# GpSimd's arithmetic of the first two layers is given to VectorE and ScalarE

## The chip, the cores and the metric

The kernel runs on one core of one Trainium2 chip. The metric is the device time of one execution in microseconds. Three runs of the kernel before took 1056.38, 1057.58 and 1059.24 us; the median is 1057.58 us.

## The reference, cut to what matters

Four layers work one after the other on x of 256 rows and 1024 columns, all in fp32. The first layer holds stick-breaking attention and a grouped state-space mixer (S5), the second a gated linear attention (GLA) in chunks of 64 rows; the third and fourth are hybrid layers with dilated attention and retention, which the change doesn't touch. What matters of the first two:

```
# layer 1: S5, 32 groups of 16 channels, 64 complex states each
lam_bar = exp(lam * dt)
b_bar   = ((lam_bar - 1) / lam)[..., None] * (b_re + i b_im)
bu      = einsum('gnp,blgp->blgn', b_bar, u)
h[t]    = lam_bar * h[t-1] + bu[t]                       # over 256 rows
y       = einsum('gpn,blgn->blgp', c_re, h.real) - einsum(..., c_im, h.imag) + d * u
y       = gelu(y);  y = y * sigmoid(y @ w_glu + b_glu)
x       = x + concat(o_sticks * silu(z_a), y * silu(z_b)) @ w_out
# layer 2: GLA, 4 heads, chunks of 64 rows
g       = cumsum(log_a, over the chunk);  g_last = g[-1]
q_dec, k_inv, k_dec = q * exp(g), k * exp(-g), k * exp(g_last - g)
o       = mask(q_dec k_inv^T) v + q_dec S;   S = exp(g_last) * S + k_dec^T v
```

## The kernel before, in words

**Projections.** Weights come from one array `in_wall_dram` in tiles of 128 by 2048 (1 MB, tile name raw, three buffers), in the order in which they are used. ScalarE copies each to a rounded fp32r tile (whi), VectorE takes the difference to the original (wlo, four pieces of 512 columns), and TensorE multiplies with both parts: `proj_a` sums 512-wide results (pa) from whi, wlo, whi per 128 rows of weights, `proj_b` 512- and 256-wide ones (pb), evacuated by ScalarE and VectorE together (zz, s_room). So every projection needs all three engines, and whi and wlo tiles have three buffers each.

**S5.** The mixer is worked in four pieces of eight groups (`s5_piece`, L1112), four rows to a step, so that a scan of 64 steps does it. First `s5_prep` makes small tables of 32 columns (s_w, s_W, s_L), and per piece angles, their sines and cosines (parts of s_room, the big S5 tile). `s5_tables` (L1080) loads 256 KB of b and c for the piece (s5bc) and makes f0 (s5f), ez and F from W, L and s5bc by `s5_tab`, two products of 256 columns each, and rho for the scan. TensorE transposes ez (s5ep), ScalarE evacuates it (s5E), TensorE makes the input states (s5vp) and a 90 degree turn (s5jp), VectorE rotates, scans (s5B) and rotates back (s5V, s5m), TensorE turns again (s5jp) and gives the outputs (s5yp). Beside it, s5gp, s5f and s5tp make the taps within four rows. The tables have one buffer each, so those of a piece follow the use of the piece before. When all four are done, 32 small DMAs on SyncE's queue gather the result (s_room<-s5Y).

**GLA.** `q_evac` and `k_evac` (L1540 and on) scale q and k by the decays (qd, kc, ki, km) and prepare copies of parts of them for the chunk borders (qi, and parts of kc and km). When all four are ready, TensorE transposes kc (gkt) and goes on with the heads.

**Order.** Fibers yield instructions; `Prog.run` always issues the one with the smallest modelled start plus the fiber's bias, so that the order of every engine is fixed when the program is built. The model's costs are in `Engine.__getattr__` (L295 to L306): a VectorE product of n columns 0.066 + 0.00104 n us, a GpSimd one 0.05 + 0.0021 n us. GpSimd's and VectorE's instructions have no effect on each other in it. On an engine the instructions run in that order, each waiting for its inputs. In the trace every instruction has line L275, so the tiles' names tell what it is.

Of the kernel before, what the change touches and what calls it, by code (L numbers as in the profile page):

```python
# [11 lines left out]
AF = mybir.ActivationFunctionType  # L12
OP = mybir.AluOpType
# [3 lines left out]
P = 128  # L17
T = 256
# [945 lines left out]
def s5_prep(g, ev, S):  # L964

    act, dve, pool, C = g.act, g.dve, g.pool, g.C
    big = ev.tile([P, 20, 32], F32, name="s5_w")
    n = [0]

    def tl():  # L970
        n[0] += 1
        return big[:, n[0] - 1, :]

    def tt(o, a, b, op=OP.mult):
        return dve.tensor_tensor(o, a, b, op=op)

    def ts(o, a, s1, s2, op0, op1=None):
        return dve.tensor_scalar(o, a, s1, s2, op0=op0, **({"op1": op1} if op1 else {}))

    lre, lim = C("lre"), C("lim")  # L980
    dt, a, th = tl(), tl(), tl()
    yield act.activation(dt, C("ldt"), AF.Exp)
    yield tt(a, lre, dt)
    yield tt(th, lim, dt)
    q, p = tl(), tl()
    r, kk = tl(), tl()
    yield from reduce_angle(g, r, th, kk)
    sn, cm1 = tl(), tl()
    f = tl()
    yield ts(f, r, 4.0 / TWO_PI, None, OP.mult)  # L990
    yield ts(kk, f, MAGIC, MAGIC, OP.add, OP.subtract)
    yield tt(f, f, kk, OP.subtract)

    jv = g.K("misc")[:, 0:64]
    flat = lambda t, b: t[:, 8 * b:8 * b + 8, :].rearrange("p a j -> p (a j)")

    def turns():
        for b in range(4):
            gs = slice(8 * b, 8 * b + 8)
            yield pool.tensor_tensor(S.cosj[:, gs, :], f[:, gs].unsqueeze(2).to_broadcast([P, 8, 64]),  # L1000
                                     jv.unsqueeze(1).to_broadcast([P, 8, 64]), op=OP.mult)
        for b in range(4):
            yield ts(flat(S.sinj, b), flat(S.cosj, b), MAGIC, MAGIC, OP.add, OP.subtract)
            yield tt(flat(S.cosj, b), flat(S.cosj, b), flat(S.sinj, b), OP.subtract)
            yield act.activation(flat(S.sinj, b), flat(S.cosj, b), AF.Sin, scale=TWO_PI_BELOW)
            yield act.activation(flat(S.cosj, b), flat(S.cosj, b), AF.Abs)
            yield act.activation(flat(S.cosj, b), flat(S.cosj, b), AF.Sin, scale=-TWO_PI_BELOW, bias=g.halfpi)
            g.flags.add(("turns", b))
        yield from rotary_tables(g)
    yield act.activation(sn, r, AF.Sin)  # L1010
    yield act.activation(cm1, r, AF.Sin, scale=0.5)
    g.spawn(turns(), 0.05)
    yield ts(q, a, -88.0, 1.0 / 256.0, OP.max, OP.mult)
    yield ts(p, q, 1.0 / 6.0, 1.0, OP.mult, OP.add)
    for i in (5, 4, 3, 2):
        yield tt(p, p, q)
        yield ts(p, p, 1.0 / i, 1.0, OP.mult, OP.add)
    yield tt(p, p, q)
    for _ in range(8):
        yield dve.scalar_tensor_tensor(p, p, 2.0, p, op0=OP.add, op1=OP.mult)  # L1020
    em1, ea, cs = p, tl(), tl()
    yield ts(ea, em1, 1.0, None, OP.add)
    yield dve.scalar_tensor_tensor(cm1, cm1, -2.0, cm1, op0=OP.mult, op1=OP.mult)
    yield ts(cs, cm1, 1.0, None, OP.add)
    xr, xi = tl(), tl()
    rho, lr1, den, u, v = S.rho, tl(), tl(), tl(), tl()
    yield tt(xr, em1, cs)
    yield tt(xi, ea, sn)
    yield tt(xr, xr, cm1, OP.add)
    yield tt(lr1, ea, cs)  # L1030
    yield tt(rho, ea, ea)
    yield tt(u, lre, lre)
    yield tt(rho, rho, rho)
    yield tt(v, lim, lim)
    L, Wt = S.L, S.W
    yield dve.tensor_copy(L[:, 0, :, 0], lr1)
    yield dve.tensor_copy(L[:, 1, :, 0], xi)
    yield tt(den, u, v, OP.add)
    yield dve.reciprocal(den, den)
    u2, v2 = tl(), tl()  # L1040
    yield tt(u, xr, lre)
    yield tt(v, xi, lim)
    yield tt(u2, xi, lre)
    yield tt(v2, xr, lim)
    yield tt(u, u, v, OP.add)
    yield tt(u2, u2, v2, OP.subtract)
    yield tt(Wt[:, 0, :, 3], u, den)
    yield tt(Wt[:, 1, :, 3], u2, den)

    def cmul(o, i):  # L1050

        j = i - 1 if o is L else i + 1
        ar, ai = o[:, 0, :, j], o[:, 1, :, j]
        yield tt(u, ar, lr1)
        yield tt(v, ai, xi)
        yield tt(u2, ar, xi)
        yield tt(v2, ai, lr1)
        yield tt(o[:, 0, :, i], u, v, OP.subtract)
        yield tt(o[:, 1, :, i], u2, v2, OP.add)

    for k in (2, 1, 0):
        yield from cmul(Wt, k)

    yield ts(Wt[:, 1], Wt[:, 1], g.sg, None, OP.mult)
    g.flags.add("s5W")
    for k in (1, 2, 3):
        yield from cmul(L, k)
    yield ts(L[:, 0], L[:, 0], g.sg, None, OP.mult)
    g.flags.add("s5L")


def s5_tab(g, bc, m, w, c):

    for a in range(2):
        w4 = w.rearrange("p (q a) t -> p q a t", a=2)[:, :, a, :].unsqueeze(3).to_broadcast([P, 4, 4, 16])
        b4 = bc[:, c, :].rearrange("p (q a c) -> p q a c", q=4, a=2)[:, :, a, :].unsqueeze(2).to_broadcast([P, 4, 4, 16])
        yield g.pool.tensor_tensor(m(a), w4, b4, op=OP.mult)


def s5_tables(g, S):  # L1080

    pool = g.pool
    for b in range(4):
        gs = slice(8 * b, 8 * b + 8)
        bc = yield from g.get("s5bc", [P, 4, P])
        yield g.sp.dma_start(out=bc, in_=g.A["s5bc"][b])
        ez = yield from g.get("s5ez", [P, 512])
        f0 = yield from g.get("s5f0", [P, P])
        yield pool.tensor_scalar(f0, bc[:, 2, :], g.sg, None, op0=OP.mult)
        if "s5W" not in g.flags:  # L1090
            yield g.on("s5W")
        m = yield from g.t2k("s5t")
        half = lambda t: lambda a: t.rearrange("p (q t a c) -> p q t a c", q=4, t=4, a=2)[:, :, :, a, :]
        yield from s5_tab(g, bc, half(ez), S.W[:, 0, gs, :], 0)
        yield from s5_tab(g, bc, half(m), S.W[:, 1, gs, :], 1)
        yield pool.tensor_tensor(ez, ez, m, op=OP.subtract)
        S.ez[b] = (ez, f0)
        rho = yield from g.get("s5rho", [P, 8, 64])
        yield pool.tensor_tensor(rho, S.rho[:, gs].unsqueeze(2).to_broadcast([P, 8, 64]),
                                 g.K("misc")[:, 64:128].unsqueeze(1).to_broadcast([P, 8, 64]), op=OP.mult)  # L1100
        if "s5L" not in g.flags:
            yield g.on("s5L")
        own = lambda t: lambda a: t.rearrange("p (q a t c) -> p q a t c", q=4, t=4, a=2)[:, :, a]
        F = yield from g.get("s5F", [P, 512])
        yield from s5_tab(g, bc, own(F), S.L[:, 0, gs, :], 2)
        yield from s5_tab(g, bc, own(m), S.L[:, 1, gs, :], 3)
        yield pool.tensor_tensor(F, F, m, op=OP.subtract)
        g.put(m, bc)
        S.fr[b] = (F, rho)


def s5_piece(g, S, Y, b):  # L1112

    act, dve, pool, pe = g.act, g.dve, g.pool, g.pe
    U = S.U
    gs = slice(8 * b, 8 * b + 8)
    r3 = lambda t: t.rearrange("p (a j) -> p a j", a=8)
    if b not in S.ez:
        yield lambda: b in S.ez
    ez, f0 = S.ez[b]  # L1120
# [5 lines left out]
    for a in range(2):  # L1126
        yield act.activation(E[:, :, a, :], ep.rearrange("p (q n) -> p q n", q=4), AF.Copy,
                             scale=g.half[:, a:a + 1])
# [43 lines left out]
    F, rho = S.fr[b]  # L1172
    yield dve.tensor_tensor_scan(B, rho.rearrange("p a j -> p (a j)"), B, 0.0, OP.mult, OP.add)
    g.put(rho)
    yield dve.tensor_tensor(r3(V), sb, r3(B), op=OP.mult)
    yield pool.tensor_tensor(r3(m), cb, r3(B), op=OP.mult)
    g.put(B)
    jp = yield from g.ps1("small", "s5jp")
    yield pe.matmul(jp, g.K("jt"), V, start=True, stop=True)
# [293 lines left out]
def odd_layer(g, od):  # L1473
# [73 lines left out]
    def q_evac(j):  # L1547
        def evac(o):
            sl = slice(2 * j, 2 * j + 2)
            if "eg" not in g.flags:  # L1550
                yield g.on("eg")
            yield dve.scalar_tensor_tensor(fl(qd[:, sl]), o, P ** -0.5, fl(eg[:, sl]), op0=OP.mult, op1=OP.mult)
            g.put(o)
            if "ed" not in g.flags:
                yield g.on("ed")
            yield pool.tensor_copy(qi[:, sl, 0:64], qd[:, sl, P:P + 64])
            for i in (2 * j, 2 * j + 1):
                yield pool.tensor_scalar(qi[:, i, 64:128], qd[:, i, P + 64:T], egl[:, 4 * i + 2:4 * i + 3], None, op0=OP.mult)
            ready.add(("q", j))
        return evac  # L1560

    def k_evac(j):
        def evac(o):
# [8 lines left out]
            yield dve.tensor_tensor(km[:, sl, :, 0:64], o4[:, :, :, 0:64], e4[:, sl, :, 0:64], op=OP.mult)  # L1572
            g.put(o)
            for i in (2 * j, 2 * j + 1):
                yield pool.tensor_scalar(kc[:, i, 0:64], kc[:, i, 0:64], egl[:, 4 * i + 1:4 * i + 2], None, op0=OP.mult)
            yield pool.tensor_copy(km[:, sl, :, 64:128], ki.rearrange("p h (a t) -> p h a t", a=2)[:, sl, :, 64:128])
            ready.add(("k", j))
        return evac
    yield from g.proj_a(g.ha, [[("ov", nb, kt) for kt in range(2)] for nb in range(2)],
# [427 lines left out]
```

## Time and profile before

| | |
|---|---|
| runs, us | 1056.38, 1057.58, 1059.24 |
| profiled execution, us | 1061.02 |
| its span, first to last instruction, us | 1059.2 |
| mean granted TensorE clock | 0.988 |
| TensorE matmuls busy, us | 1025.7 (97%), 5507 |
| VectorE busy, us | 823.5 (78%), 1807 |
| ScalarE busy, us | 556.2 (53%), 935 |
| GpSimd busy, us | 69.0 (7%), 79 |

Busy times are unions of an engine's instructions. [...] PE is TensorE, PEld its weight loads, DVE VectorE, ACT ScalarE, POOL GpSimd, SP SyncE, whose q stands for the queue that issues DMAs. An fp32 matmul shows as two. [...] GpSimd is busy only in the first 143 us and for some us around 300.

### The profile page before, as it was taken

Reading aid. Unit: us, or ns where it says so; the run is one execution under the profiler, and the core shown is the slowest. Engines: PE = TensorE matmul, PEld = TensorE weight load, DVE = VectorE, ACT = ScalarE, POOL = GpSimd, SP = SyncE. Lnnn points to the kernel's source line nnn. Section 1 sums busy time; section 2 is a strip of 40 time slices with the busy share of each in tenths; the row PEclk is TensorE's granted clock in tenths of the full one; section 3 lists DMA queues with packets and bytes.
Section 4 is the critical chain, followed back from the end, with each engine's and each line's share of the span. In section 5 each row is a group of like instructions: output and inputs, shape, how many; then the busy total and the mean of one; then the engine's idle time right before and its main releaser. Section 6 shows DMA issues by size and latency. Waiting matters only on the chain.

```text
span 1059.2 us, 14771 instructions
## 1 busy us (share of the span) xinstructions
PE 1025.7 (97%) x5507; PEld 863.3 (81%) x5507; DVE 823.5 (78%) x1807; ACT 556.2 (53%) x935; POOL 69.0 (7%) x79
## 2 busy tenths in 40 slices
PE   9978999999999999999999999999999999999997
PEld 7756777877888778888888888878888888888885
DVE  7997466977789867867599989676676759996775
ACT  7636347755645655445544556555454454455552
POOL 0266410000030000000000000000000000000000
PEclk9998899999999999999999999999999999999999
DMA  8522124454663767564444577545655453454541
GB/s 330 175 93 90 50 88 133 170 183 169 265 247 127 261 251 287 207 243 164 161 153 155 179 259 271 175 150 204 234 189 204 144 187 143 149 182 176 199 179 41
DMA packets 33492, 192.36 MB, mean 182 GB/s; under 512 B 8171, under 2 KB 9195, under 8 KB 11148
## 3 DMA queue, kind: packets, MB, share of 16 engines
q1 hardware_dynamic: 33132, 190.90, 50.1%
q8 instruction: 43, 0.70, 0.3%
q10 hardware_dynamic: 288, 0.52, 0.1%
q14 instruction: 29, 0.24, 0.1%
HBM read 189.31 MB, written 1.05 MB: 180 GB/s over the span
## 4 chain that ended last, share of the span: by engine, by line
PE 77%; DVE 12%; DMA 3%; ACT 2%; issue 2%; POOL 1%; SPq 1%; POOLq 0%; DVEq 0%; ACTq 0%
PE pb L275 46%; PE pa L275 19%; DVE wlo L275 4%; PE as L275 4%; DMA raw<-in_wall_dram 2%; PE ret L275 2%; DVE rs L275 2%; SPq L275 1%; PE sbz L275 1%; PE s5yp L275 1%; ACT whi L275 1%; PE ntp L275 1%; DVE s_w L275 1%; DVE s_room L275 1%; PE gsc L275 0%
## 5 line engine op out<-in xcount | busy, mean ns | idle before, releaser
L275 DVE TENSOR_TENSOR wlo<-raw,whi 128x512 fp32r<-128x512 f32 x604 | 399.2, 697 | 94.4 <-ACT whi L275 94.4
L275 PE MATMUL pb<-H,whi 128*128 128x512 f32 x1344 | 470.0, 400 | 0.0
L275 PE MATMUL pb<-H,wlo 128*128 128x256 f32 x1344 | 353.7, 283 | 0.0
L275 ACT ACTIVATE whi<-raw 128x1024 fp32r<-128x1024 f32 x302 | 304.7, 1052 | 73.8 <-PE pa L275 38.6
L275 PEld LDWEIGHTS pb<-H,whi 128*128 128x128 f32 x1344 | 242.6, 188 | 46.4 <-issue 1.5
L275 PEld LDWEIGHTS pb<-H,wlo 128*128 128x128 f32 x1344 | 253.6, 189 | 15.7 <-issue 0.7
L275 PE MATMUL pa<-whi,H 128*128 128x512 f32 x576 | 184.4, 397 | 2.1 <-DVE H L275 2.1
L275 PEld LDWEIGHTS pa<-whi,H 128*128 128x128 f32 x576 | 108.1, 189 | 26.6 <-DVE H L275 3.5
L275 PE MATMUL pa<-wlo,H 128*128 128x512 f32 x288 | 114.2, 397 | 1.3 <-DVE wlo L275 1.2
L275 ACT ACTIVATE zz<-pb 128x256 f32<-128x256 f32 x120 | 45.3, 381 | 121.3 <-PE pb L275 120.6
L275 PE MATMUL pb<-yy,whi 128*128 128x512 f32 x192 | 67.5, 399 | 0.2
L275 PEld LDWEIGHTS pa<-wlo,H 128*128 128x128 f32 x288 | 54.7, 190 | 13.9 <-DVE wlo L275 2.5
L275 DVE SCALAR_TENSOR_TENSOR acc<-raw,cact,acc 128x512 f32<-128x512 f32 x84 | 60.1, 747 | 4.8 <-DMA raw<-in_wall_dram 4.7
L275 DVE TENSOR_TENSOR zz<-pb,zz 128x256 f32<-128x256 f32 x120 | 49.9, 419 | 14.8 <-ACT zz L275 14.4
L275 PE MATMUL pb<-yy,wlo 128*128 128x256 f32 x192 | 48.7, 281 | 0.0
L275 PE MATMUL pa<-whi,mg 128*128 128x512 f32 (+1 forms) x144 | 41.6, 372 | 0.0
L275 PEld LDWEIGHTS pb<-yy,whi 128*128 128x128 f32 x192 | 34.7, 188 | 7.3 <-DVE tg L275 1.5
L275 PEld LDWEIGHTS pb<-yy,wlo 128*128 128x128 f32 x192 | 36.2, 189 | 2.8
L275 PE MATMUL pa<-whi,mix 128*128 128x512 f32 x96 | 30.2, 392 | 0.7 <-ACT mix L275 0.7
L275 ACT ACTIVATE sqj<-x 128x512 f32<-128x512 f32 (+1 forms) x19 | 11.5, 606 | 36.7 <-DVE x L275 32.4
L275 PEld LDWEIGHTS pa<-whi,mg 128*128 128x128 f32 x144 | 26.0, 188 | 5.0
L275 ACT ACTIVATE ka<-pb 128x256 f32<-128x256 f32 x24 | 9.2, 385 | 37.4 <-PE pb L275 37.4
(288 smaller groups left out, 1195.1 us busy)
## 6 DMA issues: line engine op xcount, KB each, us to landing
raw<-in_wall_dram SPq DMA_DIRECT2D x174, 1024.0 KB, 4.8
x<-in_x_dram SPq DMA_DIRECT2D x2, 512.0 KB, 5.1
raw<-in_wall_dram SPq DMA_DIRECT2D x2, 512.0 KB, 5.2
s5bc<-in_s5bc_dram SPq DMA_DIRECT2D x4, 256.0 KB, 3.8
gate<-in_bgate_dram SPq DMA_DIRECT2D x2, 512.0 KB, 5.8
c<-in_cst_dram SPq DMA_DIRECT2D x1, 896.0 KB, 6.6
cst<-in_cst_dram SPq DMA_DIRECT2D x1, 704.0 KB, 11.5
s_room<-s_room SPq DMA_DIRECT2D x16, 32.0 KB, 4.6
```

What stands on the lines that cost most here:

```text
L275: i.eng, i.emit = name, (lambda: real(*a, **k))
```

## The change

GpSimd's products, differences, scalings and copies of the first two layers become instructions of VectorE (the angle products, the tables' products and differences, the product m of the rotation back) or of ScalarE (f0, rho, and the copies and scalings of GLA). rho is no longer a product with a row of ones and zeros but a memset of column 0 on GpSimd and a ScalarE copy of 63 columns. GpSimd keeps memsets only. Nothing else of the code changes, but the costs that the planner sees do, so it lays out all engines anew from there; the piece loads s5bc stand in other places of SyncE's queue, too.

```
@@ s5_prep, turns()
-            yield pool.tensor_tensor(S.cosj[:, gs, :], f[:, gs].unsqueeze(2).to_broadcast([P, 8, 64]),
-                                     jv.unsqueeze(1).to_broadcast([P, 8, 64]), op=OP.mult)
+            yield dve.tensor_tensor(S.cosj[:, gs, :], f[:, gs].unsqueeze(2).to_broadcast([P, 8, 64]),
+                                    jv.unsqueeze(1).to_broadcast([P, 8, 64]), op=OP.mult)
@@ s5_tab
-        yield g.pool.tensor_tensor(m(a), w4, b4, op=OP.mult)
+        yield g.dve.tensor_tensor(m(a), w4, b4, op=OP.mult)
@@ s5_tables
-        yield pool.tensor_scalar(f0, bc[:, 2, :], g.sg, None, op0=OP.mult)
+        yield act.activation(f0, bc[:, 2, :], AF.Copy, scale=g.sg)
...
-        yield pool.tensor_tensor(ez, ez, m, op=OP.subtract)
+        yield dve.tensor_tensor(ez, ez, m, op=OP.subtract)
...
-        yield pool.tensor_tensor(rho, S.rho[:, gs].unsqueeze(2).to_broadcast([P, 8, 64]),
-                                 g.K("misc")[:, 64:128].unsqueeze(1).to_broadcast([P, 8, 64]), op=OP.mult)
+        yield pool.memset(rho[:, :, 0:1], 0.0)
+        yield act.activation(rho[:, :, 1:64], S.rho[:, gs].unsqueeze(2).to_broadcast([P, 8, 63]), AF.Copy)
...
-        yield pool.tensor_tensor(F, F, m, op=OP.subtract)
+        yield dve.tensor_tensor(F, F, m, op=OP.subtract)
@@ s5_piece
-    yield pool.tensor_tensor(r3(m), cb, r3(B), op=OP.mult)
+    yield dve.tensor_tensor(r3(m), cb, r3(B), op=OP.mult)
@@ odd_layer, q_evac
-            yield pool.tensor_copy(qi[:, sl, 0:64], qd[:, sl, P:P + 64])
+            yield act.activation(qi[:, sl, 0:64], qd[:, sl, P:P + 64], AF.Copy)
             for i in (2 * j, 2 * j + 1):
-                yield pool.tensor_scalar(qi[:, i, 64:128], qd[:, i, P + 64:T], egl[:, 4 * i + 2:4 * i + 3], None, op0=OP.mult)
+                yield act.activation(qi[:, i, 64:128], qd[:, i, P + 64:T], AF.Copy, scale=egl[:, 4 * i + 2:4 * i + 3])
@@ odd_layer, k_evac
-                yield pool.tensor_scalar(kc[:, i, 0:64], kc[:, i, 0:64], egl[:, 4 * i + 1:4 * i + 2], None, op0=OP.mult)
-            yield pool.tensor_copy(km[:, sl, :, 64:128], ki.rearrange("p h (a t) -> p h a t", a=2)[:, sl, :, 64:128])
+                yield act.activation(kc[:, i, 0:64], kc[:, i, 0:64], AF.Copy, scale=egl[:, 4 * i + 1:4 * i + 2])
+            yield act.activation(km[:, sl, :, 64:128], ki.rearrange("p h (a t) -> p h a t", a=2)[:, sl, :, 64:128], AF.Copy)
```

How the instructions move shows best on VectorE at the end of the first S5 piece, from its scan (s5B<-s5rho) to the sum that the outputs wait for (s5m<-s5jp). Before, with the product of cosines and s5B on GpSimd:

```order
L275 SCALAR_TENSOR_TENSOR s5B<-s5rho,s5B 128x512
L275 TENSOR_TENSOR qraw<-qraw,rs 128x512
L275 TENSOR_TENSOR s5V<-s_room,s5B 128x512
L275 TENSOR_SCALAR kT<-qtp,cols 128x4x128
L275 TENSOR_TENSOR wlo<-raw,whi 128x512
L275 TENSOR_TENSOR s5m<-s5jp,s5m 128x512
```

And now, from the last difference of the second piece's ez on:

```order
L275 TENSOR_TENSOR s5ez<-s5ez,s5t 128x512
L275 SCALAR_TENSOR_TENSOR s5B<-s5rho,s5B 128x512
L275 TENSOR_TENSOR qraw<-qraw,rs 128x512
L275 TENSOR_TENSOR s5V<-s_room,s5B 128x512
L275 TENSOR_TENSOR s5m<-s_room,s5B 128x512
L275 TENSOR_TENSOR qraw<-qraw,rs 128x512
L275 TENSOR_TENSOR wlo<-raw,whi 128x512
L275 TENSOR_TENSOR s5m<-s5jp,s5m 128x512
```

The product s5m<-s_room,s5B stands on VectorE behind s5V, and the ez table of the next piece is made ahead of the scan; the evacuation kT has moved behind the piece.

The second place is VectorE in the second piece, from s5f, which needs TensorE's s5gp (the taps), to the scan. Before:

```order
L275 TENSOR_TENSOR s5f_797<-s5gp,sgc 128x128
L275 TENSOR_TENSOR wlo<-raw,whi 128x512
L275 TENSOR_TENSOR s5B<-s_room,s5V 128x8x63
L275 TENSOR_TENSOR s5m<-s_room,s5jp 128x8x63
L275 TENSOR_TENSOR s5B<-s5B,s5m 128x8x63
L275 SCALAR_TENSOR_TENSOR s5B<-s5rho,s5B 128x512
```

Now:

```order
L275 TENSOR_TENSOR s5f_845<-s5gp,sgc 128x128
L275 TENSOR_TENSOR s5B<-s_room,s5V 128x8x63
L275 TENSOR_TENSOR s5m<-s_room,s5jp 128x8x63
L275 TENSOR_TENSOR s5B<-s5B,s5m 128x8x63
L275 TENSOR_TENSOR s5ez<-s_W,s5bc 128x16x16 x2
L275 TENSOR_TENSOR s5t<-s_W,s5bc 128x16x16 x2
L275 SCALAR_TENSOR_TENSOR s5B<-s5rho,s5B 128x512
```

The four products of the third piece's ez stand between the rotation and the scan, and no wlo does.

The third place is ScalarE in the second layer, around the last pb evacuations (zz) ahead of gkt. Before:

```order
L275 ACTIVATE ed<-ed 128x1024
L275 ACTIVATE whi<-raw 128x1024 x2
L275 ACTIVATE zz<-pb 128x256 x3
L275 ACTIVATE whi<-raw 128x1024 x2
L275 ACTIVATE zz<-pb 128x256 x2
L275 ACTIVATE kc<-gkt 128x512
```

Now, from the last zz but four on:

```order
L275 ACTIVATE zz<-pb 128x256 x2
L275 ACTIVATE kc<-kc,egl 128x64 x2
L275 ACTIVATE zz<-pb 128x256
L275 ACTIVATE km<-ki 128x4x64
L275 ACTIVATE whi<-raw 128x1024 x2
L275 ACTIVATE zz<-pb 128x256 x2
L275 ACTIVATE kc<-kc,egl 128x64 x2
L275 ACTIVATE km<-ki 128x4x64
L275 ACTIVATE kc<-gkt 128x512
```

The scalings of kc and the copies to km stand between the evacuations, the last two directly ahead of the evacuation of gkt.

## Rows read from the trace of the kernel before

**Rows 1.** Busy time by stretch: stretch, length, then each engine, clock, DMA share, GB/s
```profile
50.00:100.00 50.00, 36.98 (x207) 28.07 (x205) 46.49 (x90) 26.52 (x46) 33.89 (x34) 0.95 0.28 93
100.00:150.00 50.00, 47.71 (x255) 36.69 (x254) 24.16 (x43) 18.99 (x50) 19.77 (x22) 0.84 0.17 58
150.00:200.00 50.00, 48.63 (x271) 41.19 (x270) 39.70 (x81) 36.65 (x64) 0.00 (x0) 1.00 0.43 139
```

**Rows 2.** Waits from 50 to 150 us: total us, times, longest us
```profile
PE s5ep L275 <- POOL s5ez L275: 1.5, 1, 1.5
PE s5jp L275 <- ACT s5V L275: 1.4, 1, 1.4
...
PE s5vp L275 <- ACT s5E L275: 1.2, 1, 1.2
...
DVE s5m L275 <- POOL s5m L275: 2.9, 2, 1.7
```

**Rows 3.** Busy time by stretch, the three stretches at half clock
```profile
64.50:67.90 3.40, 3.07 (x11) 2.87 (x12) 3.33 (x9) 2.23 (x4) 1.97 (x4) 0.50 0.75 296
98.70:108.80 10.10, 9.78 (x33) 6.39 (x34) 3.79 (x6) 2.57 (x4) 5.34 (x8) 0.50 0.29 118
126.00:132.70 6.70, 6.70 (x33) 5.26 (x32) 2.06 (x2) 1.99 (x7) 4.37 (x7) 0.50 0.46 157
```

**Rows 4.** Instructions in order of time, TensorE: start, length, [idle before <- cause]
```profile
37.43 0.40 PE L275 MATMUL pa<-whi,H 128*128 128x512 f32 x1
...
64.83 2.08 PE L275 MATMUL s5tp<-s5f,cst 128*128 128x128 f32 x8 [2.99 <-DVE s5f L275]
...
99.02 0.66 PE L275 MATMUL s5yp<-s_room,s5T 128*128 128x64 f32 x2 [2.46 <-DVE s5m L275]
...
125.71 0.45 PE L275 MATMUL s5yp<-s_room,s5T 128*128 128x64 f32 x2 [2.04 <-DVE s5m L275]
...
148.59 0.34 PE L275 MATMUL s5yp<-s5m,s5F 128*64 128x64 f32 x4
...
152.15 0.62 PE L275 MATMUL pa<-whi,H 128*128 128x512 f32 x2
```

**Rows 5.** Groups by shape, VectorE, 50 to 100 us: busy us, mean ns, idle
```profile
L275 DVE TENSOR_TENSOR wlo<-raw,whi 128x512 fp32r<-128x512 f32 x16 | 15.9, 1011 | 1.3 <-ACT whi L275 1.3
```

**Rows 6.** Groups by shape, GpSimd, whole span
```profile
L275 POOL TENSOR_TENSOR s5ez<-s_W,s5bc 128x256 f32<-128x256 f32 x8 | 8.0, 1017 | 13.0 <-DVE s_W L275 13.0
L275 POOL TENSOR_TENSOR s5m<-s_room,s5B 128x512 f32<-128x512 f32 x4 | 7.4, 1847 | 12.9 <-DVE s5B L275 12.9
```

**Rows 7.** Instructions in order of time, VectorE, at 33 us
```profile
33.01 0.18 DVE L275 TENSOR_TENSOR s_w<-s_w 128x32 f32<-128x32 f32 x1
33.11 0.74 DVE L275 TENSOR_SCALAR qT<-qtp,cols 128x512 f32<-128x512 f32 x1
```

**Rows 8.** Instructions in order of time, VectorE, at 307 us
```profile
306.66 0.41 DVE L275 TENSOR_TENSOR kc<-zz,ed 128x256 f32<-128x256 f32 x1
307.00 0.68 DVE L275 TENSOR_TENSOR ki<-zz,ei 128x512 f32<-128x512 f32 x1
307.60 0.41 DVE L275 TENSOR_TENSOR km<-zz,ed 128x256 f32<-128x256 f32 x1
```

**Rows 9.** Instructions in order of time, VectorE, at 31 us
```profile
31.30 0.68 DVE L275 TENSOR_TENSOR qraw<-qraw,rs 128x512 f32<-128x512 f32 x1
```

**Rows 10.** Instructions in order of time, ScalarE, at 91 us
```profile
91.13 0.60 ACT L275 ACTIVATE s5T<-s5tp 128x512 f32<-128x512 f32 x1 [0.76 <-PE s5tp L275]
91.75 1.28 ACT L275 ACT_TABLE_LOAD   x1
```

**Rows 11.** Instructions in order of time, SyncE's queue
```profile
149.38 3.78 SPq L275 DMA_DIRECT2D s_room<-s5Y  x6
```

**Rows 12.** Waits of TensorE, 300 to 320 us: total us, times, longest us
```profile
PE gkt L275 <- POOL kc L275: 1.2, 1, 1.2
```

**Rows 13.** Instructions in order of time, GpSimd, at 307 us
```profile
307.17 2.67 POOL L275 TENSOR_SCALAR kc<-kc,egl 128x64 f32<-128x64 f32 x2 [3.91 <-DVE kc L275]
```

More of the change, by code (lines that the diff above doesn't have):

```diff
@@ L1076, in s5_tab @@
         b4 = bc[:, c, :].rearrange("p (q a c) -> p q a c", q=4, a=2)[:, :, a, :].unsqueeze(2).to_broadcast([P, 4, 4, 16])
-        yield g.pool.tensor_tensor(m(a), w4, b4, op=OP.mult)
+        yield g.dve.tensor_tensor(m(a), w4, b4, op=OP.mult)
 def s5_tables(g, S):
-    pool = g.pool
+    act, dve, pool = g.act, g.dve, g.pool
     for b in range(4):
```

## Prediction

> **What bounds the kernel now.** I read the stretches first, then the waits inside the bad one, then single instructions there. From 50 to 150 us TensorE is busy for 36.98 and 47.71 us of twice 50, from 150 on nearly always [rows 1]. So 15.3 us are idle there, of 33.5 in the whole span (1059.2 less the page's 1025.7 busy); the rest is spread over 950 us. Nearly all waits of that stretch belong to the four S5 pieces: the last matmuls of a piece (s5yp) wait 2.46 and 2.04 us for s5m, the tap matmuls (s5tp) 2.99 us for s5f [rows 4], the transposes (s5ep) 1.5 us for GpSimd's s5ez [rows 2]. VectorE is named for most of them, but it is late because of GpSimd in two ways: it waits for GpSimd's product s5m, 2.9 us [rows 2], and its own instructions grow while GpSimd runs. The 16 wlo differences between 50 and 100 us take 1011 ns on the mean [rows 5]; one alone, like ki at 307.00, takes 0.68 [rows 8].
>
> The granted clock is the other loss. [...] At half speed busy matmuls take twice as long, so about 10.1 us go there.
>
> **The change, part by part.** VectorE gets 32 products 256 columns wide (s5ez, s5t, s5F), 8 differences, 4 angle products and 4 products s5m, the last 16 all 512 wide. No row shows these products on VectorE. Nearest are kc and ki, which start 0.34 and 0.60 us before the next instruction [rows 8]; qraw, whose second operand is broadcast as in the tables, takes 0.68 us like an ordinary one [rows 9]. I take 32 x 0.34 + 16 x 0.60 = 20.5 us. The upper bound is GpSimd's own duration, 1.02 and 1.85 us [rows 6], so 32 x 1.02 + 16 x 1.85 = 62 us; the lower is nothing, as the growth that leaves VectorE may pay for it. Between 50 and 100 us that growth is 16 x (1.01 - 0.68) = 5.3 us for wlo alone [rows 5, 8]; with the rest of VectorE's work there and the other half of the stage I estimate two to three times that, 10 to 17 us.
>
> [...]
>
> Now the two engines' sums up to the last s5m and s5yp of the fourth piece. **VectorE**, in the new order, from the qT evacuation at 33.11 us [rows 7]: 106 instructions 504 or 512 wide, at 0.60 [rows 8], 66 us with twice that for the four scans; 42 of 256 at 0.34, 14 us; 114 of 8 or 32 columns at 0.10 [rows 7], 11 us; 8 others, some 3 us. Together 95 us, so it could be done at 128.
>
> **TensorE**: before, from its first projection matmul of the stage at 37.43 to the last s5yp at 148.93 [rows 4], 111.5 us. Less 15.3 of waits and 10.1 of slow clock that is 86.1 us of work. The new order puts 226 instead of 174 pa matmuls ahead of that s5yp; at a pitch of 0.62 - 0.40 = 0.22 us [rows 4] these 52 are 11.5 us. So the new order could be there at 37.4 + 86.1 + 11.5 = 135 us, and the old one reached the same work at 148.9 + 11.5 = 160.4. TensorE is the later of the two engines by some 7 us, which is why VectorE's 20.5 us cost nothing of their own: TensorE's extra projection matmuls hide them (94 instead of 66 pa stand ahead of the first s5ep, for instance). If that cover went, all 20.5 us less the 10 to 17 of growth would show.
>
> What is late next are the hand-overs, each in turn TensorE, ScalarE, VectorE, TensorE. Without GpSimd in them they wait 1.4 us (s5jp for ScalarE's s5V) and 1.2 us (s5vp for s5E) [rows 2]. Two places are tight: VectorE's sum to the first s5m is 42 us, so 75 us, where TensorE's is 75 too; and in the second piece s5f now stands where VectorE must wait for s5gp some 3 us, with the next table, a scan and three wlo queued behind it, but those wlo are needed only ten us later. I take 1.5 us a piece, 6 us; ends 2 and 12. As none of these waits reaches 2 us I let the clock stay up. Gain of the stage: 15.3 + 10.1 - 6 = 19.4 us.
>
> **ScalarE** gets s5f (128 wide) and s5rho (504 wide) four times, at most 0.60 each like s5T, and two more table loads at 1.28 us, since the rotary Sin now falls between the sticks [rows 10]: together under 8 us, hidden in its idle time (busy 26.5 and 19.0 of 50 us [rows 1]); uncovered they would delay a hand-over by 1.28. Four memsets of 8 columns stay on GpSimd and cost nothing that is waited for.
>
> **SP**: two raw tiles instead of one now stand between the loads of s5bc, and the gather of s5Y is issued as 6, 5, 18 and 3 with weight loads between, before as 6, 7, 9, 5 and 5. At 3.78 us for six [rows 11] eighteen hold the queue for 11 us. Three raw and three split tiles are ahead of TensorE, each worth 24 matmuls, 5.3 us; of these, two cover most of it and three all. Without any it would cost 11 us.
>
> **Second layer**: the gkt transposes wait 1.2 us for GpSimd's kc, two scalings in 2.67 us [rows 12, 13]. On ScalarE two 64-wide copies are under 0.60 each by [rows 10], behind one zz copy: the wait goes, 1.2 us, to less than the 0.3 I leave. The qi and km copies are waited for by nobody earlier.
>
> Sum: 19.4 + 0.9 = 20.3, say 20.5 us. The profiled execution took 1061.02 us with a span of 1059.2; it comes to 1040.5, and since the median of the runs, 1057.58, is 3.4 us below that execution, to 1037 us.
>
> **Rivals.**
> (a) The clock still falls. For: 20 us at half speed came with waits only a little above the ones I expect, and pieces of 64-wide matmuls remain. Against: three waits of 1.2 to 1.5 us left it up [rows 2, 3]. Then 10.1 us stay lost: 1047. [...]
> (b) VectorE becomes the bound of the stage without being ruinous: products at 0.60 instead of 0.34 us add 8 us, which uses up the 7 us of lead, and hand-overs go to 12 us with one or two falls of the clock, 5 us. Gain 20.5 - 1 - 6 - 5 = 8.5: 1049. For: VectorE is busy for 46.5 of the 50 us from 50 to 100 [rows 1]. Against: qraw [rows 9].
> (c) Slower: VectorE runs the broadcast products at GpSimd's prices, 62 us. Then its sum is 74.5 + 62 = 136.5 us, so 169.6 and with 6 us of hand-overs 175.6, against 160.4 before: 15 us later, 1072. It is slower from a mean of 1.0 us for each of the 48 moved instructions, (160.4 - 6 - 33.1 - 74.5) / 48; I take 0.43. Only the missing row speaks for it.
> (d) No change: the stage ends earlier but a later one gives it back, since the weights of the first layer's output projection must come 20 us sooner. Against: DMA is at 0.28, 0.17 and 0.43 in the three stretches [rows 1], with room. 1056.
>
> **Chances.** Forecast 0.62, with a range of its own of 1031 to 1043 (hand-overs 2 to 12 us, growth and pitch as taken); (a) 0.18; (b) 0.10; (c) 0.05; (d) 0.05. The range of 8 in 10 runs from 1029 to 1050, which takes in (a) and (b). A measurement here tells about 0.3%, 3 us, from no change: faster 0.89, within 0.04, slower 0.07.
>
> **What would show it.** In the profile after: GpSimd busy for under 2 us; wlo between 50 and 100 us at about 0.69; the s5ez products with a mean near 0.41; TensorE idle for 5 to 8 us from 50 to 150 instead of 15.3; no wait above 2 us there and a granted clock of 1.00 in both halves; the last stick's matmuls before the long pb run, which end at 186 us now, at 164 to 168; no wait of gkt. Wrong would be: a clock below 0.95 in that stage (a), VectorE products of 0.6 us and more or s5V, s5m and wlo still waited for by 2 us and more (b, c), or the stage early and raw tiles waited for after it (d).

## The result, and the profile after

The kernel after takes 1040.38 us (four runs, 1039.08 to 1042.12), against 1056.98 us before (the three runs shown above and a fourth, 1055.82 to 1059.24): a ratio of 0.9841, 95% interval 0.9819 to 0.9864. In a later session on one chip it took 1040.23 us against 1059.24 us, ratio 0.9823 (0.98 to 0.9846). The forecast was 1037 us, its range 1029 to 1050.

The profiled execution of after has a span of 1038.5 us, 20.7 less than before's. The stretches of [rows 1] again, in the same columns:

```profile
50.00:100.00 50.00, 49.06 (x277) 39.37 (x275) 47.21 (x143) 35.84 (x79) 0.45 (x4) 1.00 0.41 128
100.00:150.00 50.00, 49.50 (x312) 40.11 (x312) 39.31 (x84) 30.73 (x52) 0.23 (x2) 1.00 0.29 96
150.00:200.00 50.00, 48.13 (x260) 39.82 (x258) 43.58 (x82) 36.16 (x64) 0.00 (x0) 1.00 0.44 147
```

TensorE, in the first column after the length, is idle for 0.94 + 0.50 = 1.4 us from 50 to 150 where it was idle for 15.3, and its granted clock is 1.00 in both halves, where 20.2 us stood at 0.50 [rows 3]. The waits of [rows 4] are gone. What is left of waits there, in order of time, and behind it the waits that are new:

```profile
60.88 0.66 PE L275 MATMUL s5ep<-cst,s5ez 128*128 128x128 f32 x4 [0.48 <-DVE s5ez L275]
75.22 0.67 PE L275 MATMUL s5jp<-s5V,cst 128*128 128x512 f32 x1 [0.24 <-DVE s5V L275]
...
159.80 1.06 PE L275 MATMUL sbz<-sb_sp,vE 128*128 128x128 f32 x8
...
188.39 0.50 PE L275 MATMUL pb<-mix,whi 128*128 128x512 f32 x1 [0.68 <-DVE zz L275]
190.52 0.50 PE L275 MATMUL pb<-mix,whi 128*128 128x512 f32 x1 [0.46 <-DVE zz L275]
197.45 0.73 PE L275 MATMUL pa<-whi,mix 128*128 128x512 f32 x2 [0.70 <-DVE mix L275]
202.31 0.50 PE L275 MATMUL pa<-whi,mix 128*128 128x512 f32 x1 [2.27 <-ACT mix L275]
...
288.09 0.60 PE L275 MATMUL gkt<-cst,kc 128*128 128x128 f32 x4
```

The last stick's matmuls end at 160.9 instead of 186 us, and gkt does not wait [rows 12]. But four waits for zz and for mix (the rounded input of the output projection) stand ahead of the first layer's output projection and in it, 4.1 us together; before, one of 0.7 stood there. VectorE's groups of [rows 5], 50 to 100 us:

```profile
L275 DVE TENSOR_TENSOR wlo<-raw,whi 128x512 fp32r<-128x512 f32 x23 | 15.8, 703 | 0.0
...
L275 DVE TENSOR_TENSOR s5ez<-s_W,s5bc 128x256 f32<-128x256 f32 x6 | 2.4, 433 | 0.0
...
L275 DVE TENSOR_TENSOR s_w<-s_L,s_w 128x32 f32<-128x32 f32 x12 | 1.9, 211 | 0.0
```

A wlo is back at 0.70 us from 1.01, and the new products take 0.43. VectorE, the third column of the stretches, is busy for 86.5 us from 50 to 150 where it was busy for 70.7 [rows 1], and TensorE waits less for it.

### The profile page after: what moved, and what is told of

Same layout as the page of the kernel before. It is cut to its first block, busy times and chain, and to the rows that moved or that the text cites. A ratio compares the mean times of both kernels' runs of the same rounds, so it can differ in the third digit from the quotient of the medians.

```text
span 1038.5 us, 14764 instructions
## 1 busy us (share of the span) xinstructions
PE 1016.1 (98%) x5507; PEld 857.5 (83%) x5507; DVE 822.6 (79%) x1855; ACT 564.4 (54%) x957; POOL 1.7 (0%) x15
## 3 DMA queue, kind: packets, MB, share of 16 engines
HBM read 189.31 MB, written 1.05 MB: 183 GB/s over the span
## 4 chain that ended last, share of the span: by engine, by line
PE 78%; DVE 13%; DMA 3%; ACT 2%; issue 2%; SPq 0%; DVEq 0%; ACTq 0%
PE pb L275 47%; PE pa L275 19%; DVE wlo L275 4%; PE as L275 3%; PE ret L275 2%; DMA raw<-in_wall_dram 2%; PE sbz L275 1%; DVE rs L275 1%; ACT whi L275 1%; DVE s5B L275 1%; PE s5yp L275 1%; PE gsc L275 1%; DVE s_room L275 1%; DMA cols<-in_cols_dram 1%; DVE H L275 0%
## 5 line engine op out<-in xcount | busy, mean ns | idle before, releaser
L275 DVE TENSOR_TENSOR wlo<-raw,whi 128x512 fp32r<-128x512 f32 x604 | 393.0, 687 | 93.2 <-ACT whi L275 93.2
L275 PE MATMUL pa<-whi,H 128*128 128x512 f32 x576 | 181.8, 394 | 2.1 <-DVE H L275 2.1
```

What stands on the lines that cost most here:

```text
L275: i.eng, i.emit = name, (lambda: real(*a, **k))
```

## The experiments

Theory A was that the engines made the gain: GpSimd's instructions are slow in the chain of a piece, and VectorE's grow while GpSimd runs. The first rival, B, was that the new issue order made it, on whatever engine.

**The new order on the old engines, and the old order on the new ones.** Each moved instruction is planned as one engine's and issued to the other:

```diff
+def swap(booked, real):
+    booked.emit = real.emit
+    return booked
...
-        yield g.dve.tensor_tensor(m(a), w4, b4, op=OP.mult)
+        yield swap(g.dve.tensor_tensor(m(a), w4, b4, op=OP.mult), g.pool.tensor_tensor(m(a), w4, b4, op=OP.mult))
... (and so with every other moved instruction)
```

The first run keeps after's order and GpSimd's work. 

> The issue order of all engines is that of the kernel after, but every moved instruction runs on GpSimd again (rho as a memset and a product of 63 columns). Theory A, the engines made the gain (GpSimd's own slow products in the chain, and VectorE's instructions that grow while GpSimd runs): about 1056 us, within 4 of before; GpSimd busy for 60 to 70 us, wlo between 50 and 100 us at 0.9 to 1.0 us, TensorE idle for 10 us and more from 50 to 150 us, and a granted clock of 0.50 after waits there. Rival B, the new order made it (94 instead of 66 projection matmuls ahead of the first s5ep, so TensorE has work while the tables are made): 1040 to 1045 us, and under 4 us idle.

Measured: 1057.35 us, ratio to before 0.9989 (0.9967 to 1.0011). VectorE's group of wlo from 50 to 100 us and TensorE's longest waits from 50 to 150:

```profile
L275 DVE TENSOR_TENSOR wlo<-raw,whi 128x512 fp32r<-128x512 f32 x21 | 17.8, 871 | 0.2 <-ACT whi L275 0.2
```

```profile
PE s5yp L275 <- DVE rs L275: 3.0, 1, 3.0
PE s5yp L275 <- DVE s5m L275: 2.9, 1, 2.9
PE s5tp L275 <- DVE s5f L275: 1.8, 1, 1.8
```

The long waits are back, TensorE is idle for 10.9 us and 13.7 us stand at half clock. On the old engines the order alone is worth at most 0.3%, so B falls.

The second run has before's order and the new engines. 

> The issue order of before, planned at GpSimd's costs, but every moved instruction runs on VectorE or ScalarE. Theory A: most of the gain, 1040 to 1046 us, the clock at 1.00 from 50 to 150 us. Rival B: 1052 to 1057 us, since only 66 projection matmuls cover the first table and VectorE's queue was laid out without the products.

Measured: 1054.78 us, 0.9948 (0.9928 to 0.9968), as B said and not as A did. TensorE's waits from 50 to 150 us:

```profile
PE s5yp L275 <- DVE s5m L275: 3.6, 4, 1.8
PE s5ep L275 <- DVE s5ez L275: 2.0, 1, 2.0
PE s5ep L275 <- ACT s5Y L275: 1.5, 1, 1.5
PE pa L275 <- DVE wlo L275: 1.3, 2, 0.6
```

VectorE's instructions are as short as in after (wlo 682 ns), and still 10.7 us are idle and three stretches of 3.4 us stand at half clock. 28 fewer projection matmuls stand ahead of the first s5ep here, and TensorE reaches each hand-over before VectorE, which now carries the products, does. Neither half makes the gain: the new engines need the new order, and the order needs the engines. Whether it is TensorE's cover or VectorE's own queue, laid out without the products, that the old order lacks, this run does not tell apart.

**GpSimd's work put back beside the kernel after.** 29 products on GpSimd read constants, write a tile that nobody reads, and are waited for by nobody; the small memsets move to VectorE.

```diff
...
+        if b == 0:
+            raw.tensor_copy(tr[:, 0, 0:8], S.W[:, 0, 0:8, 0])
+            for _ in range(29):
+                raw.tensor_tensor(tr, one, two, op=OP.mult)
...
```

> The kernel after, with 29 extra products of 128x512 on GpSimd that read two constants in SBUF and that nothing waits for, from the end of the first ez table on (the memsets of 8 columns are on VectorE here). Theory A1, VectorE's instructions grow while GpSimd runs products, and that alone costs: wlo between 60 and 110 us at 0.9 to 1.0 us, VectorE late by 10 to 17 us of which its lead hides some 5, so 1046 to 1056 us with TensorE idle for 8 to 15 us from 50 to 150 us. Rival A2, the growth is hidden and only GpSimd's place in the chain cost: 1040 to 1043 us.

Measured: 1074.16 us, 1.014 (1.011 to 1.0169), far above both. The products wait only for the table W and start at 56.9 us, ahead of the first ez table and not at its end as planned. From 50 to 150 us 30.8 us stand at half clock, and TensorE is idle for 26.7 us:

```profile
PE s5tp L275 <- DVE s5f L275: 11.4, 1, 11.4
PE s5ep L275 <- DVE s5rho L275: 9.0, 1, 9.0
PE s5jp L275 <- DVE s5V L275: 6.0, 2, 5.8
```

VectorE in order of time, just behind the start of the products:

```profile
56.97 2.71 DVE L275 TENSOR_TENSOR s_w<-s_L,s_w 128x32 f32<-128x32 f32 x4
59.60 0.20 DVE L275 TENSOR_TENSOR s_L<-s_w 128x32 f32<-128x32 f32 x1
59.71 0.41 DVE L275 TENSOR_TENSOR s5ez<-s_W,s5bc 128x256 f32<-128x256 f32 x1
60.04 1.28 DVE L275 TENSOR_TENSOR s_L<-s_w 128x32 f32<-128x32 f32 x1
...
90.96 0.28 DVE L275 TENSOR_TENSOR s5f<-s5gp,sgc 128x128 f32<-128x128 f32 x1
91.16 1.22 DVE L275 SCALAR_TENSOR_TENSOR rs<-rs 128x8 f32<-128x8 f32 x1
```

GpSimd over the same stretch:

```profile
56.90 45.03 POOL L1109 TENSOR_TENSOR train<-cst 128x512 f32<-128x512 f32 x29
```

An instruction of 32 or of 8 columns takes 1.2 to 1.3 us, three times as long as one of 256 between them (0.41): what grows reads not as the work but as a wait that the row shows as part of the length. s5f, with one operand in PSUM, keeps its 0.28. What I had called growth looks like a turn to wait for: 8 columns are 1.05 us longer than in after (1.22 against 0.17), a wlo is 1.07 us longer than others of the same run (1.75 at 75.34 us against 0.68), and GpSimd starts a product every 1.55 us (45.03 / 29). This is my reading of the rows; none of them names what is waited for.

On VectorE's side it is not only products and differences of two tiles that take longer. A product with one tile and a column of scalars, in before beside GpSimd's tables (from 50 to 100 us) and in after without them:

```profile
L275 DVE TENSOR_SCALAR rot<-rot,sgc 128x256 f32<-128x256 f32 x1 | 1.4, 1353 | 0.0
```

```profile
L275 DVE TENSOR_SCALAR rot<-rot,sgc 128x256 f32<-128x256 f32 x1 | 0.4, 355 | 0.0
```

The cast in front of it, with one input, takes 705 ns in before and 296 in after.

Two more runs bear on it. With copies, which have one input, in place of the products: 

> As the run with 29 products, but 84 copies of 128x512 with one input on GpSimd in their place, at an estimated 0.6 to 0.7 us each some 55 us of GpSimd work. If any GpSimd access to SBUF makes VectorE's instructions grow: the same as there, 1046 us and more, wlo at 0.9 us or above. If it takes two inputs: 1040 to 1042 us and wlo at 0.70 us.

Measured: 1068.33 us, 1.0081 (1.005 to 1.0112), wlo 841 ns against 703 in after: one input on GpSimd's side is enough, though wlo stays below the 0.9 us that was expected. The copies take 0.83 us each and 75 us in all, not 55. And the same columns as in the 29 products, in products of 64:

```diff
...
-            for _ in range(29):
-                raw.tensor_tensor(tr, one, two, op=OP.mult)
+            for _ in range(232):
+                raw.tensor_tensor(tr[:, 0, :], g.K("misc")[:, 0:64], g.K("misc")[:, 64:128], op=OP.mult)
...
```

> As the run with 29 extra GpSimd products of 512 columns, which took 1074 us, but the same columns in 232 products of 64. If a VectorE instruction that reads only SBUF has to wait until GpSimd's running instruction has ended (theory A3): VectorE's 32-column products fall from a mean of 0.55 us and more to 0.35 or less, wlo to 0.85 or less, and the time to 1045 to 1060 us. If the two engines share a bandwidth, so that columns count (rival): 1070 us and more, wlo at 0.9 us.

Measured: 1052.79 us, 0.9937 (0.9917 to 0.9957). VectorE's groups from 50 to 100 us with products of 512 columns beside them, and then of 64:

```profile
L275 DVE TENSOR_TENSOR wlo<-raw,whi 128x512 fp32r<-128x512 f32 x14 | 12.6, 911 | 0.0
L275 DVE TENSOR_TENSOR s_L<-s_w 128x32 f32<-128x32 f32 x6 | 6.5, 1088 | 0.0
L275 DVE TENSOR_TENSOR s_w<-s_L,s_w 128x32 f32<-128x32 f32 x12 | 6.1, 551 | 0.0
```

```profile
L275 DVE TENSOR_TENSOR wlo<-raw,whi 128x512 fp32r<-128x512 f32 x20 | 14.5, 736 | 0.0
L275 DVE TENSOR_TENSOR s_w<-s_L,s_w 128x32 f32<-128x32 f32 x12 | 2.2, 232 | 0.0
L275 DVE TENSOR_TENSOR s_L<-s_w 128x32 f32<-128x32 f32 x6 | 1.8, 304 | 0.0
```

The length shrinks with GpSimd's instruction, whose mean is 1477 and then 488 ns: from 1088 to 304 ns for the same 32 columns (219 in after), so a wait for an instruction's end is what fits. On GpSimd the 232 products last 131 us instead of 45; whether they wait for VectorE or take a time that does not go with the columns, this run does not tell apart. Fewer of its columns thus run beside each of VectorE's instructions, so this run alone would not exclude a shared bandwidth; the rows of the 29 products speak against it, where 8 or 32 columns take 1.2 to 1.3 us and 256 between them 0.41.

**Parts of the change.** First the product of each piece's rotation back, alone, and then the tables alone:

```diff
-    yield pool.tensor_tensor(r3(m), cb, r3(B), op=OP.mult)
+    yield dve.tensor_tensor(r3(m), cb, r3(B), op=OP.mult)
```

> The kernel before with one edit alone: the product of cosines and s5B (s5m, four of 512 columns) runs on VectorE; the tables and all else stay on GpSimd, and the planner lays the order out anew. Theory A, the tables on GpSimd (late themselves, and holding up VectorE) cost most: 1052 to 1058 us, TensorE idle for 10 us and more from 50 to 150 us. Rival, the product m in each piece's chain is the cost: 1043 to 1050 us.

Measured: 1052.24 us, 0.9936 (0.9915 to 0.9957). The waits for s5m fall below 1 us, those for s5f (2.97) and s5ez (1.51) stay.

```diff
-        yield g.pool.tensor_tensor(m(a), w4, b4, op=OP.mult)
+        yield g.dve.tensor_tensor(m(a), w4, b4, op=OP.mult)
...
-        yield pool.tensor_tensor(ez, ez, m, op=OP.subtract)
+        yield g.dve.tensor_tensor(ez, ez, m, op=OP.subtract)
...
```

(and F's difference likewise). 

> The kernel before with the other part alone: the 32 products and 8 differences of the tables run on VectorE; s5m, rho, f0, the angle products and the second layer stay on GpSimd. Theory A: most of the gain, 1042 to 1048 us, clock at 1.00 or one short fall from 50 to 150 us. Rival, m in each piece's chain is the cost: 1052 us and more, with TensorE's s5yp waiting 2 us and more for s5m.

Measured: 1049.79 us, 0.9916 (0.9888 to 0.9944), between the two expectations: not most of the gain, and not clearly more than m alone, as the two intervals overlap. TensorE still waits 2.1 us for s5m, whose product is on GpSimd, and up to 2.5 for s5V. The clock stays at 1.00 from 50 to 150 us, but the profiled execution is the fastest of five (1048.19 us), and the others have mean clocks of 0.991 to 0.994 beside its 0.998. Both edits together: 

> Tables and s5m on VectorE together; rho, f0, the angle products and the second layer's scalings stay on GpSimd as in the kernel before, about 27 us of GpSimd work. If what is left there hardly matters: 1040 to 1043 us. If the small rest (f0 at 2.3 us each, rho at 1.8 us, waiting their turn against VectorE) still delays the taps and the scans: 1045 to 1049 us.

Measured: 1049.63 us, 0.9905 (0.9878 to 0.9932), just above the second range and no better than the tables alone. VectorE's growth is gone here (wlo 681 ns), so the growth is not the whole of the cause; how much of before's loss is VectorE's wait, and how much GpSimd's own length in the chain, no run measures. What was left on GpSimd, some 32 us of small things by its groups, is worth about as much again together with the order that is planned around it. These three runs don't part the two, for each edit changes the plan too: of the 28 projection matmuls that the new order puts ahead of the first s5ep, the tables alone bring 21, m alone none. GpSimd's f0 in this run:

```profile
L275 POOL TENSOR_SCALAR s5f<-s5bc,sgc 128x128 f32<-128x128 f32 x4 | 10.4, 2603 | 70.4 <-PE s5tp L275 32.3 <-DVE s5m L275 19.6 <-DMA s5bc<-in_s5bc_dram 18.5
```

128 columns take 2.6 us there on the mean, 0.88 in before's groups, but one of the four takes 7.10 us by itself: GpSimd may now wait its turn against a fuller VectorE, which is not shown. Against after, the two profiles differ by 3.6 us of idle TensorE from 50 to 150 us, 1.2 us at gkt, 3.4 us by two short falls of the clock and 1.3 us of waits ahead of the output projection, 9.5 of the 10.1 us between the spans. Of these, only the first two can bear on GpSimd, and no wait of the first is for the taps (s5tp); one of the two falls, at 640 us, lies far behind the last instruction that the edits touch, at some 300 us.

**The waits that are new.** They come with the order and not with the engines: from the last stick to the end of the output projection TensorE is idle for 4.5 us in after and 4.8 with after's order on the old engines, but for 1.2 us in before and 1.2 with before's order on the new ones. VectorE ahead of the wait of 2.27 us, in the kernel after (glt is the gate of S5's output, the GLU):

```profile
194.30 2.50 DVE L275 TENSOR_TENSOR wlo<-raw,whi 128x512 fp32r<-128x512 f32 x4
196.71 0.69 DVE L275 SCALAR_TENSOR_TENSOR mix<-gz,mix 128x512 fp32r<-128x512 f32 x1
197.31 0.69 DVE L275 SCALAR_TENSOR_TENSOR mix<-glt,mix 128x512 fp32r<-128x512 f32 x1
197.91 1.29 DVE L275 TENSOR_TENSOR wlo<-raw,whi 128x512 fp32r<-128x512 f32 x2
199.12 0.42 DVE L275 TENSOR_TENSOR zz<-pb,zz 128x256 f32<-128x256 f32 x1
200.12 0.69 DVE L275 SCALAR_TENSOR_TENSOR glt<-glt,y 128x512 f32<-128x512 f32 x1 [0.58 <-ACT glt L275]
```

Six wlo stand in front of the last zz, for which TensorE waits by way of glt and mix. Three versions plan such evacuations earlier, with TensorE's order unchanged (the diff is cut from the third's, y3; the first, w84, leaves y_split as it is, and y2 has larger biases; z_a is the projection that gates the sticks' output):

```diff
...
-            f = self.spawn(fold(o, b))
+            f = self.spawn(fold(o, b), early)
...
-    g.spawn(y_split())
+    g.spawn(y_split(), -0.4)
...
```

> The kernel after with the evacuations of the last two z_a blocks (bias -0.8) and of the GLU projection (bias -0.5) planned ahead of the wlo differences; TensorE's order is unchanged. If the 4.1 us that TensorE waits there for zz and mix come from VectorE's order alone: 1036 to 1038 us, with under 1.5 us of these waits. Rival, the wlo that now run later are waited for in their place: 1040 to 1042 us.

Measured: 1043.12 us, 0.9844 (0.9817 to 0.987). The split of y fell behind instead, and TensorE waited 4.06 us for it; the clock stood at 0.50 for 6.8 us from 189.0 us on.

> The kernel after, with the splits of y planned first (bias -0.8), and the last z_a block and the GLU projection at -0.4. If the waits of the run w84 came from y's splits falling behind: no wait of 4 us for mix, 1038 to 1040 us. Rival, any reordering there only moves the wait, since VectorE's work in front of the output projection is the limit: 1040 to 1043 us.

Measured: 1045.22 us, 0.9876 (0.9852 to 0.9901), with waits of 2.97 us for zz and 3.77 for mix, and 3.4 us at half clock from 201.3 us on.

> As y2 with smaller biases (-0.4 for y, -0.3 for the last z_a block and the GLU projection), which leaves more wlo differences ahead of the last GLU evacuation: 1038 to 1040 us if VectorE's order is the cause, with the waits for zz and mix under 2 us together; 1040 to 1043 us by the rival.

Measured: 1039.72 us, 0.9823 (0.9797 to 0.9849). Its two long waits:

```profile
178.66 0.47 PE L275 MATMUL pb<-H,whi 128*128 128x512 f32 x1 [2.64 <-DVE zz L275]
...
197.88 0.50 PE L275 MATMUL pa<-whi,mix 128*128 128x512 f32 x1 [1.72 <-DVE mix L275]
```

They are 4.4 us against 4.1 in after: moved, not removed, though the time alone would fit the first theory. No version beats after beyond its interval. Whether VectorE's work there is the limit or a better order exists stays open.

> The kernel after once more, as the measure for the other three on the same chip: 1039 to 1042 us; its spread tells how much the runs of before vary against it.

Measured: 1040.23 us (1039.19 to 1041.57). In the same session before ran from 1053.92 to 1061.76 us, in the first session of these experiments from 1055.45 to 1065.24, at mean granted clocks from 0.981 to 0.993; the runs of after lie within some 3 us in both of its sessions.

## Why the prediction was right, step by step

- **What bounds the stage: right.** Waits and half clock went together, 13.9 and 10.1 us. The 10.1 is half of the three stretches of [rows 3], 3.4, 10.1 and 6.7 us long, which begin within 0.4 us of the ends of the waits of 2.99, 2.46 and 2.04 us [rows 4]. It counts every matmul there as twice as long; before's trace shows that about so for 512 columns, 0.43 us from one start to the next at 130.62 us against 0.23 at 133.00, and less for s5yp, six in 1.04 us at 126.50 against 0.63 at 146.33, so it is a little high.
- **"As none of these waits reaches 2 us": the clock stayed up, but not by this reason.** It fell behind waits of 1.97 and 1.80 us in the run with before's order and the new engines, and stayed at 1.00 behind 2.46 us with the tables alone. In after no wait is longer than 0.5 us from 50 to 150 us, so (a) was not put to the test that I had in mind.
- **VectorE's new products: right.** Two of 256 columns take 0.76 us from the first start to the last end in one row of after (0.76 - 0.43 = 0.33 us from one to the next), forecast 0.34, and the 512 wide ones 0.70:

```profile
90.86 0.76 DVE L275 TENSOR_TENSOR s5ez<-s_W,s5bc 128x256 f32<-128x256 f32 x2
```

- **The hand-overs: mis-sized.** I charged 6 us; 1.4 are idle in the whole stage, where 5 to 8 were to show it, and the last stick ends at 160.9 us, before the 164 to 168. The last s5yp ends at 138.6 us, where the no-wait sum said 135.
- **"If that cover went": tested.** With before's order the cover goes, and after's time is missed by 14 us. I had allowed 3.5 to 10.5 and left out the clock, whose 10.2 us at 0.50 there cost some 5.
- **The growth: right in size, wrong in kind.** By the groups that both traces show, each against its mean in after, VectorE's instructions of before are some 15 us longer from 50 to 150 us, 7.0 of them in the 24 wlo (990 against 697 ns); I had estimated 10 to 17. But I took it for slower work. Beside the 29 products it reads as a wait per instruction, 1.05 us for 8 columns and 1.07 for 512. GpSimd's lengths are not fixed either: the same product s5rho takes from 1.04 to 1.59 us in before.
- **SP's queue: right.** The 18 issues of the gather hold it for 12.0 us, forecast 11, and TensorE waits for no raw tile:

```profile
147.57 12.03 SPq L275 DMA_DIRECT2D s_room<-s5Y  x18
```

- **Second layer: right**, 1.2 us.
- **Time given back, rival (d): it came, from another cause.** From the last stick to the end of the output projection TensorE is idle for 4.5 us instead of 1.2, for zz and mix that VectorE's order brings late, and not for weights. Some 1.4 us more are idle ahead of 50 us, where runs of the same kernel differ. Together: 13.9 + 10.1 + 1.2 - 3.3 - 1.4 = 20.5 us, and the spans differ by 20.7. That my 20.5 was met is luck: two errors of 4.6 and 4.7 us cancelled.
- **The step from profile to median: this is where the 3 us between 1037 and 1040.4 lie.** The profiled execution of before took 1061.02 us, 4 above the median of its runs; that of after took 1040.25, close to its median of 1040.38. I subtracted a difference seen from a slow execution from a median: 1061.02 - 20.5 is 1040.5. Over all sessions before spreads over 11 us, after over 3.

## What to carry to other kernels

Work on GpSimd that reads SBUF was not free here, though GpSimd had only 1.7 us of other work: beside products of 1.48 us there, VectorE instructions of 8 columns that read only SBUF took 1.22 us instead of 0.17. So count VectorE's small instructions beside it before placing work there. Moving work to another engine and laying out the order anew are one change, and in this case neither half alone made more than a third of the gain. And a gain seen between two profiles should be subtracted from the profiled execution's time, not from the median of a kernel whose runs spread by more than half the gain.

## What the runs showed of the hardware that I had not expected

- 29 products of 512 columns on GpSimd that nobody waits for cost 34 us beside the kernel after; GpSimd was busy with them for only 45.
- The clock does not follow the length of a wait alone. Before, waits of 2.04 to 2.99 us stood with falls to 0.50 [rows 3, 4]; in the run with the tables alone it stays at 1.00 behind 2.12, 2.46 and 2.20 us; in the run with before's order and the new engines it fell at 56.7, 97.7 and 121.6 us, behind waits of 1.97, 1.80 and 1.19 us. The plainest case is one wait that six traces share, for mix at the output projection, 2.26 to 2.29 us long: behind it the clock stays at 1.00 in both traces of after and in the run with 84 copies, and falls to 0.50 for 3.4 us in the runs with after's order on the old engines, with 29 products and with 232.
